# Modulation rows in half-width column groups with two selector products, and a first stage with norm sums ahead and low parts on VectorE

## The chip, the cores and the metric

The kernel runs on one NeuronCore of a Trainium2 chip. The metric is the time of one execution on the device, in microseconds (us), as the median over several runs. Five engines work side by side and are called by short names here: PE (TensorE, matrix products), DVE (VectorE), ACT (ScalarE), POOL (GpSimd) and SP (SyncE, which issues most transfers). PEld is the weight loading of PE.

## The reference

One step of a diffusion backbone with two layers, for 128 prompt tokens and 512 latent tokens of width 1024, in float32. What matters here is the modulation of each sub-layer and the first projection:

```python
def ada_modulation(cond, w_mod, b_mod):
    m = jax.nn.silu(cond) @ w_mod + b_mod
    return jnp.split(m, 6, axis=-1)

def modulate(h, shift, scale):
    return h * (1.0 + scale) + shift
...
for l in range(DEPTH):
    sh1_p, sc1_p, g1_p, sh2_p, sc2_p, g2_p = ada_modulation(cond_ctx, w_mod[l], b_mod[l])
    sh1_s, sc1_s, g1_s, sh2_s, sc2_s, g2_s = ada_modulation(cond_lat, w_mod[l], b_mod[l])
    hp = modulate(rms_norm(xp, norm_mix[l]), sh1_p, sc1_p)
    hs = modulate(rms_norm(xs, norm_mix[l]), sh1_s, sc1_s)
    # layer 0: MLA and neighbourhood attention; layer 1: grouped-query attention; then
    xp = xp + g1_p * out_p ; xs = xs + g1_s * out_s
    # FFN with sh2, sc2, g2
```

w_mod is 1024 x 6144 for each layer, so a modulation is a product of two rows (the latent and the prompt condition) with a large matrix.

## The kernel before

The 640 tokens (512 latent, 128 prompt) lie along the free axis in two halves of 320, the features on 128 partitions in eight tiles k = 0 to 7. Projections are made with three products: weights and activations are split into a high part (fp32r) and a low part, and high by high, high by low and low by high are summed (`mm3`). `unit` loads a weight block of 128 x 1024, lets ACT copy its high part, and lets DVE or POOL (argument `lo`) subtract to get the low part.

The layer-0 modulation is made in ten blocks j = 0 to 9 of 512 columns, each with two groups of columns (`MOD0`). `mod0(j, ...)` returns three pieces: two halves of row products, and an end. A half takes four of the eight k tiles; each k tile g is multiplied with its silu(condition) column pair `scol` into its own group of 32 PSUM partitions, 512 columns wide, by a matmul that uses only 32 columns of the array. After the second half ACT copies the 128 x 512 result to the tile `modsb`. The end turns it: four products of 128 columns each with `sel`, which picks and adds the four groups' rows, give `mods` with one column for each condition, and DVE adds the bias. `mkgs` then makes `gs`, the scale times the norm's weight.

The first stage makes the norm of the input and, step by step, the first three projection units wA0, wA1, wA4. For a pair of tiles k, `made(j)` runs the end of block j, `mkgs`, and `hm.make`, which gives t (`h00t`, DVE), its high part (`h00h`, ACT) and low part (`h00l`, DVE). `first` then multiplies. Of the norm, `nrm.add` sums squares on ACT and DVE into `n00acc`, and `nrm.rstd` multiplies this with ones on PE (`n00p`) and takes Ln and Exp on ACT (`n00rs`). Raw modulation rows (`mraw`) arrive in eight transfers of 1 MB. The order is written by hand: `run` queues each piece on PE behind the last matmul.

Blocks 4 to 9 stand in the neighbourhood-attention stage, one per head, as pieces m0, m1 and m2 among score, transpose and projection pieces; their raw rows arrive in quarters of 512 KB (`mod_raw`). Each fp32 matmul of the program appears as two passes in the profile, with a weight load of its own each.

Of the kernel before, what the change touches and what calls it, by code (L numbers as in the profile page):

```python
# [11 lines left out]
F32 = mybir.dt.float32  # L12
F32R = mybir.dt.float32r
AF = mybir.ActivationFunctionType
# [4 lines left out]
P = 128  # L19
# [5 lines left out]
HT = T // 2  # L25
# [23 lines left out]
def body(ctx, tc, xT, vecs, crow, wm0, wm0g, wm1, wA, wNV, wNA, wMK, wMV, wOA, wGQ, wGK, wGV, wOC,  # L49
# [3 lines left out]
    V, S, G = nc.vector, nc.scalar, nc.gpsimd  # L53
# [13 lines left out]
    main = ctx.enter_context(tc.tile_pool(name="main", bufs=1))  # L67
# [4 lines left out]
    tp = ctx.enter_context(tc.tile_pool(name="tp", bufs=4))  # L72
# [27 lines left out]
    def tmp(name):  # L100
        return tp.tile([P, T], F32, tag="t", bufs=3, name=name)

    def f(ap):
        return ap.bitcast(F32)
# [7 lines left out]
    def run(pieces):  # L112

        for piece in pieces:
            with tc.issue_after(PE.last.ins):
                piece()
# [13 lines left out]
    ident = main.tile([P, P], F32, name="ident")  # L130
# [4 lines left out]
    V.memset(eps, EPS)  # L135
    lnsc = main.tile([P, 1], F32, name="lnsc")
    V.memset(lnsc, math.log(GQA_SCALE))
    sel = main.tile([P, 2], F32, name="sel")
    V.memset(sel, 0.0)
    for g in range(4):  # L140
        V.tensor_copy(sel[32 * g:32 * g + 32, :], ident[32 * g:32 * g + 32, 32 * g:32 * g + 2])
    mods = [main.tile([P, 48, 2], F32, name=f"mods{l}") for l in range(2)]
    gs = [[main.tile([P, 8, 2], F32, name=f"gs{l}{i}") for i in range(2)] for l in range(2)]

# [3 lines left out]
    def bmod(l, j, n):  # L148
        return vec[:, V_BMOD + 48 * l + j:V_BMOD + 48 * l + j + n]

    def bc2(ap):
        return bass.AP(tensor=ap.tensor, offset=ap.offset, ap=list(ap.ap) + [[0, 2]])
# [6 lines left out]
    def load(src, n, name):  # L159
        raw = rawp.tile([P, 1024], F32, tag="raw", name=name)  # L160
        nc.sync.dma_start(raw[:, :n], src)
        return raw[:, :n]

    def unit(src, n, name, lo="v", pool=None):

        raw = load(src, n, name + "r")
        t = (pool or wp).tile([P, 2, 1024], F32R, tag="w", bufs=3, name=name)
        hi, lw = t[:, 0, :n], t[:, 1, :n]
        S.activation(hi, raw, AF.Copy)
        (V if lo == "v" else G).tensor_tensor(lw, raw, f(hi), ALU.subtract)  # L170
        return hi, lw
# [146 lines left out]
    scol = keep.tile([P, KT, 32], F32, name="scol")  # L318
# [4 lines left out]
    def mod0(j, bk, load_):  # L323

        box = []

        def part(half):
            def run():
                if half == 0:
                    box.append(bk())  # L330
                psm, rs = box[0], load_(j, half)
                for g in range(4):
                    r = rs[g // 2][:, 512 * (g % 2):512 * (g % 2 + 1)]
                    PE.matmul(psm[32 * g:32 * g + 32, :], scol[:, 4 * half + g, :], r, start=half == 0, stop=half == 1,
                              tile_position=(0, 32 * g))
                if half == 1:
                    box.append(tmp(f"modsb{j}"))
                    S.activation(box[1][:, :512], psm, AF.Copy)
            return run

        def end():
            psm, sb = box
            for i in range(4):
                PE.matmul(psm[:, 2 * i:2 * i + 2], sb[:, i * P:(i + 1) * P], sel, start=True, stop=True)
            for i, t in enumerate(MOD0[j]):
                V.tensor_tensor(mods[0][:, t:t + 2, :], psm[:, 4 * i:4 * i + 4].rearrange("p (a b) -> p a b", b=2),
                                bc2(bmod(0, t, 2)), ALU.add)
        return [part(0), part(1), end]

    def mkgs(l, i, k0=0, k1=8):  # L350
        sc = SC1 if i == 0 else SC2
        n = (V_NMIX if i == 0 else V_NFFN) + 8 * l
        V.scalar_tensor_tensor(gs[l][i][:, k0:k1, :], mods[l][:, sc + k0:sc + k1, :], 1.0, bc2(vec[:, n + k0:n + k1]),
                               ALU.add, ALU.mult)
# [114 lines left out]
    nrm = Norm("n00", D)  # L469
# [12 lines left out]
    def first(ks, us):  # L482
        for k in ks:
            for u in us:
                for c, (c0, c1) in enumerate(HALF):
                    proj(pss[u][c], *w3[u], hh, hl, [k], c0, c1, first=k == 0, last=k == KT - 1, w0=k)

    with tc.tile_pool(name="start", bufs=1) as big:
        raws = {}

        def fetch(j):
            for half in range(2):
                raws[j, half] = big.tile([P, 2, 1024], F32, tag="mraw", bufs=8, name=f"mraw{j}_{half}")
                nc.sync.dma_start(raws[j, half], wm0[j, 2 * half:2 * half + 2].rearrange("q p n -> p q n"))


        fetch(0)
        w3 = [unit(wA[0], 1024, "wA0", "g")]
        fetch(1)
        w3 += [unit(wA[i], 1024, f"wA{i}", "g") for i in (1, 4)]  # L500
        fetch(2)
        fetch(3)
        m = [mod0(j, lambda j=j: bank(f"mod{j}", "m"), lambda j, half: [raws[j, half][:, q, :] for q in range(2)]) for j in range(4)]

        def made(j):

            m[j][2]()
            mkgs(0, 0, 2 * j, 2 * j + 2)
            for k in (2 * j, 2 * j + 1):
                for i in range(2):  # L510
                    hm.make(i, nrm.rs, k)

        def rows(j):
            return m[j][:2]

        rows(0)[0]()
        run(rows(0)[1:] + [lambda i=i: nrm.rstd(i) for i in range(2)])
        run([lambda: made(0)] + rows(1))
        run([lambda: first((0, 1), [0]), lambda: made(1), lambda: first((0, 1), [1, 2])])
        run(rows(2))  # L520
        run([lambda: first((2, 3), [0]), lambda: made(2), lambda: first((2, 3), [1, 2])])
        run(rows(3))
        run([lambda: first((4, 5), [0]), lambda: made(3), lambda: first((4, 5), [1, 2])])
        run([lambda u=u: first((6, 7), [u]) for u in range(3)])
    sb = ExitStack()
# [46 lines left out]
    for kk in range(4):  # L572
        wh, wl = unit(wNV[kk], 1024, f"wnv{kk}")
        for j in range(2):
            k = 2 * kk + j
            a, b = wh[:, 512 * j:512 * (j + 1)], wl[:, 512 * j:512 * (j + 1)]
# [246 lines left out]
    for h in range(8):  # L823
        p, r = divmod(h, 2)
# [41 lines left out]
    sb = ExitStack()  # L866
# [60 lines left out]
    for h in range(8):  # L927
        p, r = divmod(h, 2)
# [390 lines left out]
    box, nxt = next_mod("h01", gs[0][1], mods[0], SH2, (op[5], op[1]))  # L1319
# [8 lines left out]
    sb = ExitStack()  # L1328
# [197 lines left out]
    box, nxt = next_mod("h11", gs[1][1], mods[1], SH2, (op[5], op[1]))  # L1526
# [168 lines left out]
```

## Time and profile before

| | |
|---|---|
| runs | 1556.8, 1561.05, 1561.08 us; median 1561.05 |
| profiled execution | 1557.29 us, span 1555.5 us, mean granted clock 0.99 |
| PE busy | 1491.6 us, 96% of the span |
| DVE, ACT, POOL busy | 1110.7, 740.8, 236.9 us |
| moved by DMA | 212.97 MB, mean 137 GB/s, 367 GB/s in the first of 40 slices |
| row products `mod<-mraw,scol` | 160 passes, 24.3 us busy, mean 648 ns of one |
| selector products `mod<-sel,modsb` | 80 passes |

Times in the profile are microseconds from the span's start. A row of the timeline has the start, the duration, the engine, the line of the kernel, the operation, out<-in tiles, and in brackets how long the engine was idle before and what ended it. Neighbouring rows of one kind are merged with a count, so a duration is then that of the run of them. In the names of tiles buffer numbers are left out (`wA` is wA1 or wA4, `h00h` any k).

### The profile page before, as it was taken

How to read it: one execution, taken by the hardware profiler on the slowest of the kernel's cores; microseconds unless marked ns; L12 is line 12 of the kernel's file. 1: busy time of each engine (PE TensorE's matmuls, PEld its weight loads, DVE VectorE, ACT ScalarE, POOL GpSimd, SP SyncE). 2: the span in 40 equal slices, each digit the busy share in tenths (PEclk: the TensorE clock that was granted, in tenths of full speed). 3: DMA queues.
4: the chain of work that ended last, by engine and by line, in shares of the span. 5: the costliest groups of instructions: out<-in, count | busy, mean ns of one | idle time of the engine just before them, and what ended most of it. 6: DMA issues, size and time to landing. Idle time of an engine off the chain costs nothing.

```text
span 1555.5 us, 25420 instructions
## 1 busy us (share of the span) xinstructions
PE 1491.6 (96%) x9868; PEld 1424.2 (92%) x9868; DVE 1110.7 (71%) x2068; ACT 740.8 (48%) x1420; POOL 236.9 (15%) x306
## 2 busy tenths in 40 slices
PE   5999989989999999999999999999989999999997
PEld 3888878879899999999999889989889999999997
DVE  5556676885779988865997787775879977743333
ACT  5445576773645555541223556663645555531221
POOL 1215444432100000000002433222100000000000
PEclk8999999999999999999999999999999999999999
DMA  9234541004165555558763211003165544457311
GB/s 367 88 112 133 176 137 57 28 14 140 36 221 180 179 170 170 168 201 320 240 227 125 88 43 35 34 15 95 38 204 186 173 133 133 143 207 264 89 41 68
DMA packets 73097, 212.97 MB, mean 137 GB/s; under 512 B 8096, under 2 KB 12976, under 8 KB 72720
## 3 DMA queue, kind: packets, MB, share of 16 engines
q1 hardware_dynamic: 70640, 205.89, 40.1%
q10 hardware_dynamic: 1920, 4.52, 0.9%
q8 instruction: 77, 1.26, 0.4%
q0 software_dynamic: 416, 0.93, 0.2%
q14 instruction: 44, 0.36, 0.1%
HBM read 182.86 MB, written 28.46 MB: 136 GB/s over the span
## 4 chain that ended last, share of the span: by engine, by line
PE 75%; DVE 12%; ACT 5%; DMA 5%; issue 2%; POOL 0%; ACTq 0%; DVEq 0%; POOLq 0%
PE fg L61 15%; PE fo L61 10%; PE fd L61 7%; PE fu L61 4%; PE gq L61 2%; PE nq L61 2%; PE mod L61 2%; PE nk L61 2%; PE go L61 1%; PE fo_2b L61 1%; PE fo_4b L61 1%; PE fo_2a L61 1%; PE fo_6b L61 1%; PE fo_4a L61 1%; PE fo_6a L61 1%
## 5 line engine op out<-in xcount | busy, mean ns | idle before, releaser
L1302 DVE SCALAR_TENSOR_TENSOR junk<-wm,cb 128x1024 bf16<-128x1024 f32 x112 | 136.7, 1220 | 21.4 <-DMA wm<-in_wm 8.4
L244 POOL TENSOR_SCALAR h10h<-h10t,gs,mods 128x320 fp32r<-128x320 f32 x4 | 5.5, 1385 | 434.8 <-DVE h10t L238 432.7
L61 PE MATMUL gq<-h10h,wgq 128*128 128x320 f32 x256 | 65.7, 315 | 0.2
L61 PE MATMUL fg<-h01q,wgu 128*128 128x320 f32 x240 | 49.6, 316 | 0.9 <-DVE h01q L287 0.4
L1065 ACT ACTIVATE wZ<-s 128x1024 fp32r<-128x1024 f32 x35 | 37.1, 1059 | 24.0 <-PE fd L61 15.7
L1065 ACT ACTIVATE wY<-s 128x1024 fp32r<-128x1024 f32 x35 | 37.1, 1060 | 22.7 <-PE fg L61 19.6
L1134 DVE TENSOR_TENSOR sg<-up,sg 128x640 f32<-128x640 f32 x35 | 28.8, 823 | 26.0 <-ACT sg L1133 26.0
L61 PEld LDWEIGHTS gq<-h10h,wgq 128*128 128x128 f32 x256 | 44.7, 188 | 1.5 <-PE gtp L65 1.0
L312 DVE SCALAR_TENSOR_TENSOR xr<-fo,mods,xr 128x320 f32<-128x320 f32 (+2 forms) x48 | 19.6, 436 | 35.0 <-PE fo L61 34.8
L1066 DVE TENSOR_TENSOR wZ<-s,wZ 128x1024 fp32r<-128x1024 f32 x35 | 42.8, 1222 | 2.4
L1066 DVE TENSOR_TENSOR wY<-s,wY 128x1024 fp32r<-128x1024 f32 x35 | 42.7, 1219 | 0.3
L61 PE MATMUL fg<-h11q,wgu 128*128 128x320 f32 x192 | 40.7, 321 | 0.9 <-DVE h11q L287 0.4
L61 PEld LDWEIGHTS fg<-h01q,wgu 128*128 128x128 f32 x240 | 38.1, 188 | 3.6 <-DVE h01q L287 2.1
L1472 ACT ACTIVATE gp<-gs,gb,rq 128x640 f32<-128x640 f32 (+1 forms) x40 | 31.9, 797 | 20.0 <-DVE gb L1471 17.1
L61 PE MATMUL mod<-mraw,scol 128*32 128x512 f32 x160 | 24.3, 648 | 17.1 <-DMA mraw<-in_wm 17.1
L61 PE MATMUL gq<-h10l,wgq 128*128 128x320 f32 x128 | 39.4, 308 | 0.0
L1133 ACT ACTIVATE sg<-fg 128x320 f32<-128x320 f32 x35 | 15.3, 438 | 46.5 <-PE fg L61 46.5
L61 PE MATMUL fg<-h11E,wW 128*128 128x320 f32 x216 | 34.7, 310 | 0.0
L61 PE MATMUL fd<-h11q,wZ 128*128 128x320 f32 x216 | 34.6, 309 | 0.0
L61 PE MATMUL fg<-h11q,wX 128*128 128x320 f32 x216 | 34.6, 309 | 0.0
L61 PE MATMUL fg<-h11N,wZ 128*128 128x320 f32 x216 | 34.6, 309 | 0.0
L61 PE MATMUL fu<-h11q,wX 128*128 128x320 f32 x216 | 34.6, 309 | 0.0
(3054 smaller groups left out, 5360.0 us busy)
## 6 DMA issues: line engine op xcount, KB each, us to landing
wm<-in_wm SPq DMA_DIRECT2D x48, 512.0 KB, 4.2
mraw<-in_wm SPq DMA_DIRECT2D x24, 512.0 KB, 4.1
mraw<-in_wm SPq DMA_DIRECT2D x8, 1024.0 KB, 15.3
wm<-in_wm0g SPq DMA_DIRECT2D x8, 512.0 KB, 4.9
x<-in_xT SPq DMA_DIRECT2D x8, 320.0 KB, 5.6
xr<-in_xT SPq DMA_DIRECT2D x8, 320.0 KB, 5.6
cb<-in_crow ACTq DMA_DIRECT2D x2, 1024.0 KB, 7.0
gt<-in_rpbp SPq DMA_DIRECT2D x8, 240.0 KB, 3.6
```

Source lines behind the costliest of these rows:

```text
L61: cls.last = nc.tensor.matmul(*a, **k)
L244: G.tensor_scalar(h[:, c0:c1], t, self.gsl[:, k, 0:1], self.ml[:, self.sh + k, 0:1], ALU.mult, ALU.add)
L312: V.scalar_tensor_tensor(xo[:, c0:c1], ps[:, c0 - o:c1 - o], ml[:, g + n, c:c + 1], xi[:, c0:c1], ALU.mult, ALU.add)
L1065: S.activation(t[:, 0, :], src, AF.Copy)
L1066: V.tensor_tensor(t[:, 1, :], src, f(t[:, 0, :]), ALU.subtract)
L1133: last = S.activation(sg[:, 0:HT], g[:, :HT], AF.Silu, scale=-1.0)
L1134: V.tensor_tensor(sg, up, sg, ALU.mult)
L1302: V.scalar_tensor_tensor(junk, raw, 1.0, cb[:, c, :], ALU.mult, ALU.mult, accum_out=mods[l][:, j0 + i, c:c + 1])
L1472: S.activation(dst, src, AF.Exp, bias=nb, scale=rq[:, j:j + 1], accum_out=ll[:, j:j + 1])
```

## The change

The four k tiles of a half no longer have a group of 32 partitions each. Column group b (0 or 1) of 256 columns and the parity of k give the group: 64 b + 32 (k mod 2). So each of the four groups receives two k tiles per half, in eight matmuls of 256 columns where there were four of 512. The result is 128 x 256; ACT copies half as many columns, into a smaller kind of tile, and two selector products replace four, with a `sel` of four columns (two conditions for two column groups).

In the first stage the norm sums `n00p` now stand ahead of the first block's row products (before: behind both halves), and the low parts of wA0, wA1 and wA4 are made by DVE instead of POOL.

```diff
-    sel = main.tile([P, 2], F32, name="sel")
+    sel = main.tile([P, 4], F32, name="sel")
...
-        V.tensor_copy(sel[32 * g:32 * g + 32, :], ident[32 * g:32 * g + 32, 32 * g:32 * g + 2])
+        V.tensor_copy(sel[32 * g:32 * g + 32, g // 2 * 2:g // 2 * 2 + 2], ident[32 * g:32 * g + 32, 32 * g:32 * g + 2])
...
                 for g in range(4):
-                    r = rs[g // 2][:, 512 * (g % 2):512 * (g % 2 + 1)]
-                    PE.matmul(psm[32 * g:32 * g + 32, :], scol[:, 4 * half + g, :], r, start=half == 0, stop=half == 1,
-                              tile_position=(0, 32 * g))
+                    for b in range(2):
+                        o = 512 * (g % 2) + 256 * b
+                        rows = slice(64 * b + 32 * (g % 2), 64 * b + 32 * (g % 2) + 32)
+                        PE.matmul(psm[rows, :256], scol[:, 4 * half + g, :], rs[g // 2][:, o:o + 256], start=half == 0 and g < 2,
+                                  stop=half == 1 and g > 1, tile_position=(0, rows.start))
                 if half == 1:
-                    box.append(tmp(f"modsb{j}"))
-                    S.activation(box[1][:, :512], psm, AF.Copy)
+                    box.append(tp.tile([P, HT], F32, tag="u", bufs=7, name=f"modsb{j}"))
+                    S.activation(box[1][:, :256], psm[:, :256], AF.Copy)
...
-            for i in range(4):
-                PE.matmul(psm[:, 2 * i:2 * i + 2], sb[:, i * P:(i + 1) * P], sel, start=True, stop=True)
+            for i in range(2):
+                PE.matmul(psm[:, 4 * i:4 * i + 4], sb[:, i * P:(i + 1) * P], sel, start=True, stop=True)
...
-        w3 = [unit(wA[0], 1024, "wA0", "g")]
+        w3 = [unit(wA[0], 1024, "wA0")]
         fetch(1)
-        w3 += [unit(wA[i], 1024, f"wA{i}", "g") for i in (1, 4)]
+        w3 += [unit(wA[i], 1024, f"wA{i}") for i in (1, 4)]
...
-        rows(0)[0]()
-        run(rows(0)[1:] + [lambda i=i: nrm.rstd(i) for i in range(2)])
+        nrm.rstd(0)
+        run([lambda: nrm.rstd(1)] + rows(0))
```

On PE, from its first product on, before (names with their numbers; `mod_230` is block 0, `mod_278` block 1):

```order
L61 MATMUL mod_230<-mraw_0_199,scol 32x512 x4
L61 MATMUL mod_230<-mraw_1_201,scol 32x512 x4
L61 MATMUL n00p_241<-n00acc,ones 128x320
L61 MATMUL n00p_245<-n00acc,ones 128x320
L61 MATMUL mod_230<-sel,modsb_239 128x2 x4
L61 MATMUL mod_278<-mraw_0_208,scol 32x512 x4
L61 MATMUL mod_278<-mraw_1_210,scol 32x512 x4
L61 MATMUL wA0a<-h00h_174,wA_205 128x320
```

and after (`mod_238` is block 0, `mod_284` block 1):

```order
L61 MATMUL n00p_230<-n00acc,ones 128x320
L61 MATMUL n00p_234<-n00acc,ones 128x320
L61 MATMUL mod_238<-mraw_0_199,scol 32x256 x8
L61 MATMUL mod_238<-mraw_1_201,scol 32x256 x8
L61 MATMUL mod_238<-sel,modsb_255 128x4 x2
L61 MATMUL mod_284<-mraw_0_208,scol 32x256 x8
L61 MATMUL mod_284<-mraw_1_210,scol 32x256 x8
L61 MATMUL wA0a<-h00h_174,wA_205 128x320
```

The norm sums moved ahead of block 0; the raw rows of block 1 still stand ahead of the first projection product.

On DVE, from the first gs to the second, before (`wA_205` is wA0, `wA_214` wA1, `wA_219` wA4; `h00t_256` and the like are t of one k and half):

```order
L353 SCALAR_TENSOR_TENSOR gs_100<-mods_98,vec 128x4
L230 SCALAR_TENSOR_TENSOR h00t_256<-x_0_114,gs_100,n00rs 128x320
L230 SCALAR_TENSOR_TENSOR h00t_260<-x_0_114,gs_100,n00rs 128x192
L230 SCALAR_TENSOR_TENSOR h00t_260<-x_0_114,gs_100,n00rs 128x128
L235 SCALAR_TENSOR_TENSOR h00l_182<-h00t_256,mods_98,h00h_174 128x320
...
L235 SCALAR_TENSOR_TENSOR h00l_183<-h00t_271,mods_98,h00h_175 128x128
L346 TENSOR_TENSOR mods_98<-mod_278,vec 128x4 x2
L353 SCALAR_TENSOR_TENSOR gs_100<-mods_98,vec 128x4
L230 SCALAR_TENSOR_TENSOR h00t_308<-x_2_118,gs_100,n00rs 128x320
```

and after:

```order
L357 SCALAR_TENSOR_TENSOR gs_100<-mods_98,vec 128x4
L231 SCALAR_TENSOR_TENSOR h00t_262<-x_0_114,gs_100,n00rs 128x320
L231 SCALAR_TENSOR_TENSOR h00t_266<-x_0_114,gs_100,n00rs 128x192
L171 TENSOR_TENSOR wA_205<-wA0r,wA_205 128x1024
L236 SCALAR_TENSOR_TENSOR h00l_182<-h00t_262,mods_98,h00h_174 128x320
...
L236 SCALAR_TENSOR_TENSOR h00l_183<-h00t_277,mods_98,h00h_175 128x128
L171 TENSOR_TENSOR wA_214<-wA1r,wA_214 128x1024
L350 TENSOR_TENSOR mods_98<-mod_284,vec 128x4 x2
L357 SCALAR_TENSOR_TENSOR gs_100<-mods_98,vec 128x4
L171 TENSOR_TENSOR wA_219<-wA4r,wA_219 128x1024
L231 SCALAR_TENSOR_TENSOR h00t_320<-x_2_118,gs_100,n00rs 128x320
```

The three low parts (L171) moved from POOL into DVE's row: one within the first pair of k, one ahead of the second block's mods, one behind its gs.

On ACT, behind the squares of the norm, before (`modsb_239`, later `modsb_255`, is block 0's copy):

```order
L338 ACTIVATE modsb_239<-mod_230 128x512
L211 ACTIVATE n00rs<-n00p_241,eps 128x320
L169 ACTIVATE wA_205<-wA0r 128x1024
L212 ACTIVATE n00rs<-n00rs 128x320
L211 ACTIVATE n00rs<-n00p_245,eps 128x320
L212 ACTIVATE n00rs<-n00rs 128x320
```

On ACT after, from the same place on:

```order
L212 ACTIVATE n00rs<-n00p_230,eps 128x320
L213 ACTIVATE n00rs<-n00rs 128x320
L212 ACTIVATE n00rs<-n00p_234,eps 128x320
L213 ACTIVATE n00rs<-n00rs 128x320
L342 ACTIVATE modsb_255<-mod_238 128x256
L170 ACTIVATE wA_205<-wA0r 128x1024
```

The copy of block 0 now stands behind all of the norm's Ln and Exp, and is half as wide.

More of the change, by code (lines that the diff above doesn't have):

```diff
@@ L342, in end @@
             psm, sb = box
-            for i in range(4):
-                PE.matmul(psm[:, 2 * i:2 * i + 2], sb[:, i * P:(i + 1) * P], sel, start=True, stop=True)
+            for i in range(2):
+                PE.matmul(psm[:, 4 * i:4 * i + 4], sb[:, i * P:(i + 1) * P], sel, start=True, stop=True)
             for i, t in enumerate(MOD0[j]):
-                V.tensor_tensor(mods[0][:, t:t + 2, :], psm[:, 4 * i:4 * i + 4].rearrange("p (a b) -> p a b", b=2),
+                V.tensor_tensor(mods[0][:, t:t + 2, :], psm[:, 0:8].rearrange("p (a i b) -> p a i b", a=2, b=2)[:, :, i, :],
                                 bc2(bmod(0, t, 2)), ALU.add)
```

## Prediction

> **What bounds the kernel now.** I read the page first, then the timeline of the first 60 us with all engines, then a table of stretches with the granted clock, then the modulation blocks in the attention stage, and last the chain of waits.
>
> ```profile
> PE 1491.6 (96%) x9868; PEld 1424.2 (92%) x9868; DVE 1110.7 (71%) x2068; ACT 740.8 (48%) x1420; POOL 236.9 (15%) x306
> L61 PE MATMUL mod<-mraw,scol 128*32 128x512 f32 x160 | 24.3, 648 | 17.1 <-DMA mraw<-in_wm 17.1
> ```
>
> TensorE (PE) is busy for 96% of the span and everything else is mostly under it, so a microsecond taken off PE, or off a wait of PE, is a microsecond off the time. Most of PE's idle time lies at the start, and that is where the change works. The timeline there (start, duration, engine, line, out<-in, count):
>
> ```profile
> 9.00 4.51 DVE L204 TENSOR_TENSOR n00acc<-n00acc,n00sq 128x320 f32<-128x320 f32 x11
> 14.23 1.94 PE L61 MATMUL mod<-mraw,scol 128*32 128x512 f32 x8 [14.23 <-DMA mraw<-in_wm]
> 16.69 1.60 PE L61 MATMUL mod<-mraw,scol 128*32 128x512 f32 x8 [0.52 <-DMA mraw<-in_wm]
> 18.21 1.34 PE L61 MATMUL n00p<-n00acc,ones 128*128 128x320 f32 x4
> 18.36 0.60 ACT L338 ACTIVATE modsb<-mod 128x512 f32<-128x512 f32 x1 [6.03 <-PE mod L61]
> 19.40 0.95 PE L61 MATMUL mod<-sel,modsb 128*128 128x2 f32 x8
> 20.44 0.23 DVE L346 TENSOR_TENSOR mods<-mod,vec 128x4 f32<-128x4 f32 x2 [6.93 <-ACT n00rs L211]
> 20.54 0.16 PEld L61 LDWEIGHTS mod<-mraw,scol 128*32 128x32 f32 x8 [0.28 <-DMA mraw<-in_wm]
> 20.61 2.35 POOL L170 TENSOR_TENSOR wA<-wA0r,wA 128x1024 fp32r<-128x1024 f32 x1 [19.30 <-ACT wA L169]
> 20.70 2.28 DVE L353 SCALAR_TENSOR_TENSOR gs<-mods,vec 128x4 f32<-128x4 f32 x1
> 23.09 1.07 PE L61 MATMUL mod<-mraw,scol 128*32 128x512 f32 x8 [1.49 <-DMA mraw<-in_wm]
> 23.09 1.15 DVE L230 SCALAR_TENSOR_TENSOR h00t<-x,gs,n00rs 128x320 f32<-128x320 f32 x3
> 24.29 0.41 PE L61 MATMUL wA0a<-h00h,wA 128*128 128x320 f32 x1
> 26.51 1.14 DVE L235 SCALAR_TENSOR_TENSOR h00l<-h00t,mods,h00h 128x320 fp32r<-128x320 f32 x3
> 28.08 0.47 PE L61 MATMUL wA0b<-h00l,wA 128*128 128x320 f32 x1
> 28.35 0.47 PE L61 MATMUL wA0b<-h00h,wA 128*128 128x320 f32 x1
> 28.61 1.70 PE L61 MATMUL mod<-sel,modsb 128*128 128x2 f32 x8
> 30.17 0.61 PE L61 MATMUL wA1a<-h00h,wA 128*128 128x320 f32 x1
> 31.03 3.67 DVE L230 SCALAR_TENSOR_TENSOR h00t<-x,gs,n00rs 128x320 f32<-128x320 f32 x4
> 35.99 1.92 PE L61 MATMUL mod<-mraw,scol 128*32 128x512 f32 x16
> 37.84 0.41 PE L61 MATMUL wA0a<-h00h,wA 128*128 128x320 f32 x1
> 39.41 0.31 PE L61 MATMUL wA0b<-h00l,wA 128*128 128x320 f32 x1
> 39.55 0.31 PE L61 MATMUL wA0b<-h00h,wA 128*128 128x320 f32 x1
> 39.70 0.95 PE L61 MATMUL mod<-sel,modsb 128*128 128x2 f32 x8
> 40.51 0.39 PE L61 MATMUL wA1a<-h00h,wA 128*128 128x320 f32 x1
> 41.02 0.16 DVE L353 SCALAR_TENSOR_TENSOR gs<-mods,vec 128x4 f32<-128x4 f32 x1
> ```
>
> Three things stand in these rows. The tiny gs at 20.70 lasts 2.28 us while POOL makes a low part (20.61 to 22.96); the same instruction at 41.02, with POOL idle, takes 0.16 us. So POOL's work holds DVE up. The first wA0 product cannot start before the raw rows that land at 23.09 have gone through PE (1.07 us), whatever DVE does. And the step from one projection product to the next is 0.27 us at 28.08, but 0.14 us at 39.41: PE runs at half speed there. The stretches confirm it (length, PE busy, granted clock, DMA share, GB/s):
>
> ```profile
> 17.81:21.23 3.42, 3.23 (x24) 1.00 1.03 410
> 21.23:24.64 3.41, 1.79 (x13) 1.00 1.03 410
> 24.64:28.05 3.41, 3.23 (x10) 0.50 1.03 410
> 31.47:34.88 3.41, 3.41 (x15) 0.50 1.02 406
> 34.88:38.29 3.41, 3.41 (x27) 1.00 1.03 383
> ```
>
> After a stretch with PE busy for 1.79 of 3.41 us the clock is 0.50, for 10.24 us (24.64 to 34.88), and full again after a stretch filled by products alone. In between lie stalls on h00h and h00l, and the selector products at 28.61, which move two columns each. DMA is full here, so the landings at 14.23, 16.69 and 23.09 stay.
>
> **The change, part by part.**
>
> *Norm sums first.* n00acc is ready at 13.51 (9.00 + 4.51). Two products on it take 1.34 us at full clock, about 2.3 at half. They now delay the first raw rows (landed 14.23), and both halves follow back to back: about 18.6 instead of 18.29 (16.69 + 1.60). The rstd pair is then done by about 17.5 and no longer sits between copy and scaling. With the shorter copy (0.45 assumed for 0.60) and four selector passes, gs comes at about 20.2 and lasts 0.16; h00t starts at 20.4, not 23.09.
>
> *Low parts by DVE.* This removes 2.35 us each from POOL, which nothing else waits for here, and adds three instructions to DVE:
>
> ```profile
> L170 DVE TENSOR_TENSOR wnv<-wnv0r,wnv x1: 1225/1225/1225, 68.3 to 68.3; 128x1024 fp32r<-128x1024 f32 x1
> ```
>
> So 1.23 us each. Block one on DVE is four triples of 1.15 (rows at 23.09 and 26.51) plus 1.23, 5.8 us: 20.4 to 26.2, where it ended at 27.65 before. PE starts at about 24.15 (0.15 earlier) and has twelve products: 12 x 0.27 = 3.2 gives 27.4 at half clock; at full clock DVE limits it to about 26.6. Before: 28.61. Gain 1.2 to 2.0, taken 1.6.
>
> *Selectors of block one.* From 28.61 to 30.17 eight passes cost 1.56. Four cost 0.78 at half clock, 0.40 at full. Gain 0.8 to 1.15, taken 1.0.
>
> *Next 24 products* (30.17 to 35.99, 5.82 us). At full clock 24 x 0.146 = 3.5. The low part of wA4 now stands on DVE behind those of wA1 and the second gs and ends near 30, which only the last products need. If the clock comes back one stretch after PE's work is dense, near 28, the 24 take about 3.7; if only near 31.5, 12 x 0.27 + 12 x 0.146 = 4.9. Gain 0.9 to 2.3, taken 2.1. Queued behind the low parts on DVE are h00t and h00l of block two: the four h00t that took 3.67 us under POOL need about 1.6 then, which pays for the 1.23 ahead of them. What is late next is the third pair of raw rows, landing near 31 by the 410 GB/s, just when PE comes for it.
>
> *Selectors of blocks two and three.* 39.70 to 40.51 is 0.81; half of it twice is 0.8.
>
> The start sums to 3.7 to 6.3 us, taken 5.5.
>
> *Attention stage, six blocks.* PE there:
>
> ```profile
> 145.80 1.68 PE L61 MATMUL mod<-mraw,scol 128*32 128x512 f32 x8
> 147.41 0.41 PE L61 MATMUL nq<-h00h,wnq 128*128 128x320 f32 x1
> 214.02 1.05 PE L61 MATMUL mod<-mraw,scol 128*32 128x512 f32 x4 [0.65 <-DMA mraw<-in_wm]
> 215.00 0.39 PE L61 MATMUL no<-nts_2h,nv 128*128 128x256 f32 x1
> 215.81 1.02 PE L61 MATMUL mod<-sel,modsb 128*128 128x2 f32 x8
> 217.59 0.33 PE L61 MATMUL npp2o<-npp2pth,nv 128*128 128x128 f32 x1 [0.77 <-ACT npp2pth L366]
> ```
>
> Five of six selector sets stand in a busy PE stream: 5 x 0.4 = 2.0. The last is followed by a wait for another copy, so it yields nothing. Raw rows come here in quarters. Where the second quarter is late (145.80, with 1.61 us to the next product, and 214.02) it now spreads over four column groups instead of two, so the tail of 0.98 (214.02 to 215.00) falls to about 0.55: 2 x 0.43 = 0.9. Some of the 2.9 turns into waits on ACT and DVE; bounds 1.0 and 2.9, taken 2.5. The shorter copies (L338) save nothing by themselves: ACT is 48% busy.
>
> *Row products.* The array streams as many columns as before: 16 passes of 512 take 1.85 us (35.99 to 37.84), although one lasts 648 ns, so four groups run at once; twice as many of 256 stream equally long. Eight weight loads go out within 0.16 us (20.54), 0.02 each, so more starts cost little. Lower bound nothing; upper bound, if the sixteen added loads of a block were not hidden at all, 16 x 0.02 = 0.32, or 2.6 us on the eight blocks on the path; taken 0.05 a block, 0.4, since the full overlap at 35.99 is the same kind of work.
>
> The Trainium skill, "TensorEngine Tiling (Array Packing)", Performance Considerations, Instruction Overhead, says that each matmul has about 60 cycles of overhead and warns against tiling a dimension that is small. By it the sixteen more passes of a block would cost an estimated 16 x 25 ns = 0.4 us, the whole selector gain, and the sum would be 4.8 us instead of 7.6. The 0.16 us for eight loads does not agree with it.
>
> *Sum.* 5.5 + 2.5 - 0.4 = 7.6 us. The profiled execution took 1557.29 (span 1555.5 and 1.8 around it), so 1549.7 against itself. The three timed runs are 1556.8, 1561.05 and 1561.08; the mean of all four is 1559.1, and I predict from that, **1551.5 us**.
>
> The Trainium skill, "TensorE: Matmul & The Clock Gate", Part 1: The HAM clock gate, says that a free-running window of 3.4 us decides on half or full clock, so its phase is drawn anew in each run. The trace agrees on the length (10.24 us is three of 3.41), and here one mostly idle stretch, not a wholly idle one, sufficed to lose the clock.
>
> **Rivals.**
>
> *More passes cost what they add* (for: twice the starts and weight loads; against: the row at 35.99, where the loads of the second half hide under the first). At 0.32 us a block the sum is 5.5 + 2.5 - 2.6 = 5.4: 1553.7 from the mean. The overhead rule of the Trainium skill cited above is of this kind.
>
> *The clock eats it.* PE now does less between 17.8 and 24.6 (norm sums moved ahead, half the selectors), so the clock may fall a stretch earlier and stay low until 34.9 as before. Then block one gains 1.2, selectors 0.8, the 24 products at 0.27 nothing (24 x 0.27 = 6.5 against 5.82, a loss of 0.6), later selectors 0.8: 2.2, and with 1.5 from attention 3.7, or 1555.4 and no difference against a median of 1561 that a measurement of this kernel tells (0.3% is 4.7 us). For it: the row 21.23:24.64. Against: dense products from 24.15 fill the stretch to 28.05, which stalls and selectors broke up before.
>
> *Slower: the column groups no longer overlap.* The new order goes round groups 0, 2, 1, 3 twice, with two matmuls for each group in one half. If a group's second pass had to start before the next group's first, the eight matmuls of a half would take nine steps of 0.21 = 1.9 instead of 1.0 us. On 17 halves (five at the start, twelve in attention) that is 15 us: 1559.1 + 15 - 8 = 1566. It decides from 0.47 us per half on. Against: two quarters that arrive apart are handled at 145.80 without such a chain, and 16 passes at 35.99 overlap fourfold across two halves.
>
> **How the numbers follow.** Chances: the forecast 0.66, passes that cost 0.11, clock 0.15, slower 0.06, and 0.02 for something else that leaves it even. The range runs from 6.3 + 2.9 off the fastest run with one half-clock stretch fewer (1.7 us), about 1546, to the smallest sum, 3.7 + 1.0 - 0.8, off the slowest pair, about 1557. Faster by over 0.3%: the forecast and most of the second case, 0.76; within 0.3%: the rest of it, the clock case and the remainder, 0.18; slower 0.06.
>
> **What would show it.** Right: gs at 20.2 lasting about 0.16; the first wA0 product near 24.15; the first wA0 product after the third block's raw rows near 33.5 instead of 37.84; fewer us at granted clock 0.50 before 40; selector sets of x4 with 0.4 us; a half of row products at 1.0 us with x16. Wrong: row halves of 1.3 us or more, PE waiting on DVE's h00l or on a low part for over 1 us between 25 and 32, half clock up to 35, or the early lead lost again at a DMA wait before 240.

## The result, and the profile after

The changed kernel takes 1550.74 us (median; 1550.31 to 1555.74), the kernel before 1561.01 in the same comparison. The ratio, which goes by the means (1551.86 and 1560.10), is 0.9947, 95% interval 0.9933 to 0.9961, about 8.3 us faster; the medians lie 10.3 us apart. The profiled execution took 1550.99 us (span 1549.2) against 1557.29 (1555.5). The page of after has:

```profile
PE 1485.5 (96%) x9988; PEld 1425.0 (92%) x9988; DVE 1109.3 (72%) x2071; ACT 738.6 (48%) x1420; POOL 230.0 (15%) x303
```

PE is busy 6.1 us less, and the span is 6.3 us shorter. The start of after, in the timeline (same columns as before):

```profile
13.17 2.50 PE L61 MATMUL n00p<-n00acc,ones 128*128 128x320 f32 x4 [13.17 <-DVE n00acc L205]
15.60 3.11 PE L61 MATMUL mod<-mraw,scol 128*32 128x256 f32 x32
18.79 0.38 ACT L342 ACTIVATE modsb<-mod 128x256 f32<-128x256 f32 x1 [2.06 <-PE mod L61]
20.20 0.16 DVE L357 SCALAR_TENSOR_TENSOR gs<-mods,vec 128x4 f32<-128x4 f32 x1
20.39 0.88 DVE L231 SCALAR_TENSOR_TENSOR h00t<-x,gs,n00rs 128x320 f32<-128x320 f32 x2
23.87 0.41 PE L61 MATMUL wA0a<-h00h,wA 128*128 128x320 f32 x1
24.70 1.14 DVE L236 SCALAR_TENSOR_TENSOR h00l<-h00t,mods,h00h 128x320 fp32r<-128x320 f32 x3
26.29 0.50 PE L61 MATMUL mod<-sel,modsb 128*128 128x4 f32 x4
26.65 0.39 PE L61 MATMUL wA1a<-h00h,wA 128*128 128x320 f32 x1
27.83 0.42 PE L61 MATMUL wA1a<-h00h,wA 128*128 128x320 f32 x1 [0.35 <-DVE wA L171]
28.03 1.23 DVE L171 TENSOR_TENSOR wA<-wA4r,wA 128x1024 fp32r<-128x1024 f32 x1
29.17 1.60 DVE L231 SCALAR_TENSOR_TENSOR h00t<-x,gs,n00rs 128x320 f32<-128x320 f32 x4
30.95 1.93 PE L61 MATMUL mod<-mraw,scol 128*32 128x256 f32 x32
32.82 0.41 PE L61 MATMUL wA0a<-h00h,wA 128*128 128x320 f32 x1
34.68 0.50 PE L61 MATMUL mod<-sel,modsb 128*128 128x4 f32 x4
35.04 0.39 PE L61 MATMUL wA1a<-h00h,wA 128*128 128x320 f32 x1
```

The tiny gs lasts 0.16 us, the four h00t 1.60 instead of 3.67, a selector set takes 0.36 us up to the next product (34.68 to 35.04) instead of 0.81, and the first product behind the third block's raw rows starts at 32.82 instead of 37.84. Thirty-two row passes of 256 columns take as long as sixteen of 512 did (1.93 at 30.95, 1.92 at 35.99). The stretches of before, with the granted clock in the third column from the end:

```profile
21.23:24.64 3.41, 1.93 (x25) 1.19 (x22) 3.41 (x9) 1.71 (x5) 0.00 (x0) 1.00 1.03 410
24.64:28.05 3.41, 2.92 (x18) 2.25 (x17) 2.66 (x9) 2.82 (x5) 0.00 (x0) 1.00 1.03 410
31.47:34.88 3.41, 3.41 (x43) 2.65 (x35) 2.09 (x7) 1.02 (x3) 0.00 (x0) 1.00 1.02 404
```

There is no half clock at the start of this execution from its first clock record, at 18.05, on. Further on I followed the lead, that is how much earlier the same first product of a tile starts than in the first profile of before. It is 5.92 us at ckv0a (53.32), 10.78 at mpp2t (312.94) and 10.83 at fu_3a (444.21), only 4.27 at fu_3b (457.27), and 6.29 at the end. So the lead grew well beyond the forecast in the attention stage, and over half of it was given back within 13 us at the start of the first FFN. There the rows of after are:

```profile
435.72 1.91 ACT L1295 ACTIVATE cb<-cb 128x2048 f32<-128x2048 f32 x1 [5.20 <-DMA cb<-in_crow]
445.56 1.23 DVE L1306 SCALAR_TENSOR_TENSOR junk<-wm,cb 128x1024 bf16<-128x1024 f32 x1 [2.58 <-DMA wm<-in_wm0g]
448.38 1.22 DVE L171 TENSOR_TENSOR wgu<-wgu_31r,wgu 128x1024 fp32r<-128x1024 f32 x1
449.65 3.03 PE L61 MATMUL fu_3a<-h01q,wgu 128*128 128x320 f32 x10 [4.00 <-DVE wgu L171]
```

and that of before:

```profile
456.32 1.72 PE L61 MATMUL fu_3a<-h01q,wgu 128*128 128x320 f32 x10
```

DVE ran these instructions in the order of the program. A product of a modulation tile (junk<-wm,cb) waited 2.58 us for its transfer, and behind it stood the low part of wgu_31, for which PE waited 4.00 us; half clock followed. In the first profile of before the same products had no wait.

### The profile page after: what moved, and what is told of

The parts are those of the page before. It is cut to its first block, busy times and chain, and to the rows that moved or that the text cites. A ratio compares the mean times of both kernels' runs of the same rounds, so it can differ in the third digit from the quotient of the medians.

```text
span 1549.2 us, 25659 instructions
## 1 busy us (share of the span) xinstructions
PE 1485.5 (96%) x9988; PEld 1425.0 (92%) x9988; DVE 1109.3 (72%) x2071; ACT 738.6 (48%) x1420; POOL 230.0 (15%) x303
## 4 chain that ended last, share of the span: by engine, by line
PE 78%; DVE 11%; ACT 6%; DMA 3%; issue 2%; POOL 0%; DVEq 0%; ACTq 0%; POOLq 0%
PE fg L61 16%; PE fo L61 10%; PE fd L61 8%; PE fu L61 4%; PE gq L61 2%; PE nk L61 2%; PE nq L61 1%; PE go L61 1%; PE mod L61 1%; PE fo_2b L61 1%; PE fo_4b L61 1%; PE fo_2a L61 1%; PE fo_4a L61 1%; PE fo_6b L61 1%; PE fo_6a L61 1%
## 5 line engine op out<-in xcount | busy, mean ns | idle before, releaser
L1171 ACT ACTIVATE p<-fd 128x320 f32<-128x320 f32 x35 | 15.3, 438 | 40.4 <-PE fd L61 40.3
```

The costliest lines, as they stand in the source:

```text
L1171: S.activation(p5, b5[:, :HT], AF.Copy)
```

## The experiments

Two times within each trace carry most of the readings: the lead at ckv0a, which is the work of the start, and the time from the first product of ckv0a to that of mpp2t, which holds the attention stage. In it every execution has two or three half-clock stretches of 3.41 us (6.8 or 10.2 us in all), in other places each time. Since PE works through most of them, I take half of their length off ("corrected"). This is an estimate, but little hangs on it: without it the means of the five stages with wide groups and of the seven with half-width groups are 263.1 and 259.2 us, with it 259.0 and 255.0.

| kernel | ratio to before (95%) | lead at ckv0a | ckv0a to mpp2t, corrected | fu_3a to fu_3b |
|---|---|---|---|---|
| before | 1 | 0 | 264.48 - 5.12 = 259.36 | 6.49 |
| before_again | 0.9994 (0.9983 to 1.0006) | -0.27 | 259.23 | 8.01 |
| fill_before | 1.0000 (0.9991 to 1.0009) | -1.40 | 258.06 | 10.21 |
| c_only | 0.9983 (0.9970 to 0.9995) | 1.81 | 258.83 | 12.66 |
| b_c | 0.9970 (0.9958 to 0.9982) | 3.28 | 259.69 | 10.48 |
| a_attn | 0.9995 (0.9985 to 1.0004) | 0.52 | 255.37 | 10.55 |
| a_only | 0.9969 (0.9957 to 0.9981) | 0.56 | 255.46 | 11.18 |
| a_b | 0.9953 (0.9938 to 0.9968) | 2.82 | 255.68 | 12.99 |
| a_c | 0.9946 (0.9932 to 0.9960) | 4.93 | 254.85 | 10.93 |
| after | 0.9947 (0.9933 to 0.9961) | 5.92 | 259.61 - 5.12 = 254.49 | 13.05 |
| copy_twice | 0.9960 (0.9946 to 0.9974) | 4.22 | 257.20 | 12.16 |
| after_p1 | 0.9921 (0.9906 to 0.9937) | 6.17 | 254.34 | 6.50 |
| after_l01 | 0.9921 (0.9907 to 0.9935) | 5.86 | 255.06 | 6.49 |

The lead at ckv0a also holds the clock of each execution's start, and that differs. The second table has, for each start, the engine of the low parts, the start of the first wA0 product, and the time of the 24 products of wA1 and wA4 that stand between the second selector set and the third block's raw rows, with the part of it at half clock:

| kernel | low parts by | first wA0 product | 24 products | of it at half clock |
|---|---|---|---|---|
| before | POOL | 24.29 | 5.82 | 4.71 |
| before_again | POOL | 25.34 | 5.09 | 3.10 |
| fill_before | POOL | 25.33 | 7.59 | 6.83 |
| a_only | POOL | 24.14 | 8.07 | 6.51 |
| a_attn | POOL | 25.75 | 5.96 | 0 |
| a_b | POOL | 25.64 | 5.33 | 0 |
| c_only | DVE | 23.88 | 5.72 | 3.41 |
| b_c | DVE | 23.46 | 5.17 | 3.27 |
| a_c | DVE | 23.66 | 4.38 | 0 |
| after | DVE | 23.87 | 4.30 | 0 |
| copy_twice | DVE | 24.97 | 3.69 | 0 |
| after_p1 | DVE | 23.83 | 4.31 | 0 |
| after_l01 | DVE | 23.65 | 4.27 | 0 |

Four of these stretches as the profile has them (before, a_only, c_only, after; start and end, length, busy time of PE, PEld, DVE, ACT and POOL, granted clock, DMA share, GB/s):

```profile
30.17:35.99 5.82, 5.82 (x26) 5.63 (x26) 5.50 (x11) 1.65 (x4) 3.12 (x2) 0.60 1.03 407
28.13:36.20 8.07, 6.49 (x27) 5.90 (x26) 7.78 (x13) 2.63 (x6) 4.68 (x2) 0.60 1.02 404
28.60:34.32 5.72, 5.49 (x26) 5.04 (x25) 5.68 (x14) 2.35 (x5) 0.00 (x0) 0.70 1.02 406
26.65:30.95 4.30, 3.95 (x26) 3.50 (x25) 4.27 (x10) 2.01 (x5) 0.00 (x0) 1.00 1.02 406
```

So both count. At full clock the 24 products take 5.3 to 6.0 us with low parts by POOL and 3.7 to 4.4 with low parts by DVE; with low parts by DVE, half clock over some 3.3 us of them makes that 5.2 to 5.7.

**a_attn: half-width groups in the attention stage alone.**

```diff
+        narrow = j >= 4
...
                 for g in range(4):
+                    if not narrow:
                         r = rs[g // 2][:, 512 * (g % 2):512 * (g % 2 + 1)]
...
+                        continue
+                    for b in range(2):
...
```

> The kernel before, with the half-width column groups and two selector products only in the six blocks of the attention stage (the four blocks of the first stage keep four groups of 512 and four selectors). Theory of the parts: the attention stage gives what my sum had, 2.5 us (1.0 to 2.9), so about -2.5 us. Rival from the trace of the changed kernel, where the lead over before grew from 5.9 us at 53 us to 12.3 at 244 us: the stage alone gives about 6 us, so -6 us, unless that is lost again at the DMA waits near 440 us (then -1 to -3 at the end, with 6 at 244 us). Rival of the clock: the lead gained in the stage came from half-clock stretches that happened to lie otherwise; then the lead at the same instruction, less what half-clock stretches cost, is 2 to 3 us.

The stage became 4.0 us shorter (corrected, 255.37 against 259.36), not 2.5, and not by the place of half-clock stretches. At the end no clear gain is left (ratio 0.9995, where about 2.5 us were expected): 4.1 us went at fu_3a, and another 3.1 between 486 and 697 us, where PE waited 3.4 us in all for ACT's and DVE's work on later FFN weights (0.55 in after). Why these waits come in some executions is not settled.

More important was a by-product. The start of this kernel is that of before, and in this execution its clock was full from 25.99 on. The lead at ckv0a is only 0.5 us, but that is not the price of the clock: the raw rows of block one ran at half pace here (3.64 us for 16 passes from 22.18), so the first wA0 product came 1.46 us later than in before. From that product to the third block's raw rows it took 9.79 us, against 11.70 in before and 10.97 in before_again, so full clock is worth some 1.2 to 1.9 us there. The rows of what held it up all the same:

```profile
29.28 2.35 POOL L174 TENSOR_TENSOR wA<-wA1r,wA 128x1024 fp32r<-128x1024 f32 x1 [5.65 <-ACT wA L173]
30.09 1.57 DVE L370 SCALAR_TENSOR_TENSOR gs<-mods,vec 128x4 f32<-128x4 f32 x1
31.59 2.39 POOL L174 TENSOR_TENSOR wA<-wA4r,wA 128x1024 fp32r<-128x1024 f32 x1
31.69 0.42 PE L61 MATMUL wA1a<-h00h,wA 128*128 128x320 f32 x1 [1.28 <-POOL wA L174]
34.03 0.55 PE L61 MATMUL wA<-h00h,wA 128*128 128x320 f32 x2 [0.47 <-POOL wA L174]
29.58:35.54 5.96, 4.21 (x26) 3.50 (x25) 5.65 (x8) 1.75 (x5) 4.40 (x2) 1.00 1.02 416
```

The 24 products take 5.96 us at full clock (last row, a stretch), where the first profile of before had 5.82 mostly at half: at full clock PE waits for the low parts of wA1 and wA4, which POOL makes one behind the other. My prediction had found nobody waiting for POOL there; in the profile that it read, the half clock hid the wait.

**a_only, b_c: the halves of the change.** a_only has the half-width groups everywhere and the old first stage, b_c the new first stage and the wide groups. The diff is that from the changed kernel to a_only; b_c is the kernel before with the same lines changed the other way.

```diff
-        w3 = [unit(wA[0], 1024, "wA0")]
+        w3 = [unit(wA[0], 1024, "wA0", "g")]
...
-        w3 += [unit(wA[i], 1024, f"wA{i}") for i in (1, 4)]
+        w3 += [unit(wA[i], 1024, f"wA{i}", "g") for i in (1, 4)]
...
-        nrm.rstd(0)
-        run([lambda: nrm.rstd(1)] + rows(0))
+        rows(0)[0]()
+        run(rows(0)[1:] + [lambda i=i: nrm.rstd(i) for i in range(2)])
```

> The kernel before, with the half-width groups and two selectors in all ten blocks, but the norm sums behind the first block's halves and low parts by POOL as before. Theory of the parts: the start gives only its selectors, 1.0 + 0.8, and not the 3.7 of POOL and of the clock, so the lead at 53 us is 1 to 2 us; with the attention stage (as in the run of that stage alone) -4 to -8 us there. Rival, passes cost: the lead at 53 us is below 0.5. Rival, the selectors alone keep the clock: no half-clock stretch from 24.6, lead at 53 us 4 to 6 us.

> The kernel before, with the norm sums first and the low parts by DVE, and the wide groups with four selectors everywhere. Theory of the parts: wA0's twelve products 1.6 and the next 24 products 2.1, so the lead at 53 us is 3.5 us (2 to 4), no more after it, and -3.5 us at the end. Rival, the clock decides and the selectors decide the clock: eight two-column passes a block leave PE idle enough that the half-clock stretch from 24.6 us stays; then the lead is 1.0 to 1.5 us. Rival, POOL decides all: 5.5 us as in the full change.

At ckv0a a_only has 0.56 us, less than the 1 to 2 expected: PE waits 1.6 us at 30.57 for wA1's low part, and the half clock from 29.69 to 36.52 stands over the rest of the 24 products, which take 8.07 us. b_c has 3.28, as expected, and nothing more in the attention stage. The two give 3.8 at ckv0a, the full change 5.92. That they need each other is not shown by this: both had half clock over the 24 products, after had none. At the end each is about 4.7 us faster than before, with intervals of 1.9 us either way, so their sum is no less than the 8.3 us of the full change.

**fill_before: PE kept busy before 23 us.**

```diff
-        run([lambda: made(0)] + rows(1))
+        run([lambda: made(0), rows(1)[0], filler, rows(1)[1]])   # filler: four products 128 x 192
```

> The kernel before, with four fp32 products of 128 x 192 put on PE between the two row halves of block one, into columns that nobody reads: PE is kept busy in its idle 1.5 us before 23.09, and nothing else is changed. Theory of the clock (a stretch of 3.41 us with PE busy for 1.79 brings half clock): the stretch is now busy for about 3 us, the clock stays full from 24.64, and although PE has more to do the lead at 53 us is 2 to 4 us. Rival (PE waits for h00h and h00l there anyway, whatever its clock): lead between -0.5 and 0.5 us.

The half clock came all the same, only later (30.44 to 37.27), and the lead is -1.40 us, outside both expectations. The 24 products, all but their start at half clock, took 7.59 us. So keeping PE busy before 23 us did not keep the clock, and what a full clock is worth this run cannot tell.

**a_c, a_b: one part of the first stage put back.** Of the lines in the last diff, a_c has the `rstd` lines put back, so the old place of the norm sums, and a_b the `unit` lines, so the low parts on POOL.

> The changed kernel with only the order of the norm sums put back (behind the first block's row halves); half-width groups, two selectors and low parts by DVE stay. Theory of the low parts (from the run with wide groups everywhere but the six attention blocks: with the clock full from 26 us on, PE still waited 1.3 us for POOL's low part of wA1 and 0.5 for that of wA4, and the 24 products still took 5.96 us): the low parts carry the start, the norm order only DVE's first start; gs comes near 21.9 instead of 20.2, DVE's first block ends near 27.8 instead of 26.2, so the lead at 53 us falls from 5.9 by 1.5 to about 4.4 us, and the time is 1.5 us above the changed kernel's. Rival, the raw rows at 23 us bound PE anyway: the lead stays at 5.5 to 5.9 and the order is worth nothing.

> The changed kernel with only the three low parts put back to POOL; half-width groups, two selectors and the norm sums first stay. Theory of the low parts: wA1's and wA4's low parts, 2.35 us each on POOL one behind the other, end about 5 us behind the copies of their high parts and hold PE up, and h00t of block two takes 3.67 us again; the 24 products take about 6 us whatever the clock, the lead at 53 us falls from 5.9 to about 2 us (1 to 3), and the time is 3 to 4 us above the changed kernel's. Rival of my prediction (the clock that is kept full carries 2.1 us of it and POOL only 1.6): if the clock stays full the lead is about 4.3 us.

The norm order is worth 1.0 us at ckv0a (no half clock in either start) and nothing that the end shows. With the low parts on POOL the lead is 3.1 us smaller (5.92 - 2.82), but 1.8 of that stands there before the first wA0 product (25.64 against 23.87): a_b's second half of raw rows landed later (23.78 against 22.87) and ran at half clock (20.78 to 27.61). The part that the clock does not touch is the 24 products, which with the clock full take 5.33 us in a_b and 4.30 in after, so 1.0 us. The rows of a_b:

```profile
20.27 3.58 DVE L231 SCALAR_TENSOR_TENSOR h00t<-x,gs,n00rs 128x320 f32<-128x320 f32 x4
30.20 0.41 PE L61 MATMUL wA1a<-h00h,wA 128*128 128x320 f32 x1 [0.63 <-POOL wA L171]
28.74:34.07 5.33, 4.22 (x27) 3.50 (x26) 5.01 (x8) 1.19 (x4) 3.76 (x2) 1.00 1.02 402
```

At the end a_b is about 1 us behind the changed kernel (0.9953 against 0.9947, less than the intervals), where 3 to 4 were expected.

**c_only: the low parts alone**, the `unit` lines of the first stage without the argument "g" and nothing else.

> The kernel before with only the three low parts moved from POOL to DVE; wide groups, four selectors and norm sums behind block 0 stay. With half-width groups the same move gave 4.93 - 0.56 = 4.4 us of lead at 53 us (without the norm order) and 5.92 - 2.82 = 3.1 (with it). Theory of the low parts (it is the main term of the start by itself): a lead of 2.0 to 3.5 us at 53 us, and 2 to 4 us at the end. Rival (the terms need each other: without the shorter selectors the move only passes the wait on): below 1 us.

1.81 us at ckv0a, a little under the range, and 2.7 us at the end (0.9983). With the half-width groups the same move gives 4.4 (4.93 - 0.56), but this difference holds the clock too: the 24 products of a_only ran mostly at half clock, those of c_only for 3.41 us, those of a_c at full. Whether the low parts pay more once the selectors are shorter stays open.

**copy_twice: a longer copy.**

```diff
                     S.activation(box[1][:, :256], psm[:, :256], AF.Copy)
+                    S.activation(box[1][:, :256], psm[:, :256], AF.Copy)
```

> The changed kernel, with ACT's copy of each modulation block made twice, so that it takes about as long as the old 512-wide one (0.6 us) or a little longer. My prediction said that the shorter copies save nothing by themselves. Theory from the traces: ahead of the selectors PE waited 0.36 us after the last product before and 0.12 after in three sets of the attention stage, 1.19 and 0.94 in a fourth, so PE waits for the copy and the second copy costs 0.3 us in four to six of the six sets there and some 0.3 at the start: 1.5 to 2 us less lead at 323 us than the changed kernel, and about that at the end. Rival (the prediction): nothing, within 0.5 us at 323 us.

The lead at mpp2t falls from 10.78 to 6.37: 1.7 us are lost at the start and 2.2 to 2.7 in the attention stage (257.20 against a mean of 255.04 with single copies, or 254.49 in after). The loss at the start proves little, as half clock stood there from 22.07 to 28.90. In the attention stage PE's waits ahead of the six selector sets sum to 3.46 us, against 1.21 in after. It is more than expected because another ACT instruction slipped between the two copies:

```profile
136.27 0.39 ACT L342 ACTIVATE modsb<-mod 128x256 f32<-128x256 f32 x1 [0.39 <-PE mod L61]
136.68 0.48 ACT L675 ACTIVATE nk<-nk 64x384 fp32r<-64x384 f32 x1
137.19 0.38 ACT L343 ACTIVATE modsb<-mod 128x256 f32<-128x256 f32 x1
137.63 0.61 PE L61 MATMUL mod<-sel,modsb 128*128 128x4 f32 x4 [0.75 <-ACT modsb L343]
```

So the size is that of a copy ending 0.9 us later, but the dependence is shown: PE stands still until the copy is there.

**before_again: a second profile of before.**

> The kernel before once more, unchanged, for a second profile of it. In the first one PE did not wait ahead of fu_3a (454 us), where all five other profiles have a wait of 2.0 to 4.0 us and a half-clock stretch behind it. Theory: that profile was a lucky execution by about 4 us (1557.3 against a median of 1560 to 1561), and this one shows a wait of about 2 us there. Rival: the kernel before has no wait there, and every other kernel has it because its PE comes earlier; then there is none here and the time is near 1557.

PE waits there now, in the list of waits:

```profile
PE fu_4a L61 <- DVE wgu L170: 1.9, 1, 1.9
PE fu_3a L61 <- DVE wgu L170: 1.3, 1, 1.3
```

The wait belongs to before too, and its size changes from one execution to the next. The first profile, with 1.5 at fu_4a alone, was a lucky one. But this one, at 1557.07, is no slower, so its luck at fu_3a does not explain the 1557.3.

**after_p1: one tile fewer ahead of wgu_31.**

```diff
-                    lambda kind, i: (0, 0, 0, 2, 3)[i] if kind == "fb" and i < 5 else ...
+                    lambda kind, i: (0, 0, 0, 1, 4)[i] if kind == "fb" and i < 5 else ...
```

> The changed kernel with one number pair of a plan changed: of the modulation tiles that DVE makes from loaded rows in the first FFN, one instead of two stands in step three and four instead of three in step four. In the changed kernel's trace two of them, held up by a late transfer, stand ahead of wgu_31's low part on DVE, and PE waits 4.0 us for it at 449.65 and then runs 6.8 us at half clock. Theory: the wait falls below 1.5 us and the half-clock stretch goes, so 3 to 5 us faster than the changed kernel (about 1546 to 1547.5). Rival: the wait moves to the next step (fu_4a, where four tiles now stand), and the time stays within 1 us of the changed kernel's.

1548.1 us, 2.6 under the changed kernel, a little less than expected (3 to 5). DVE comes to wgu_31 at once, PE runs on, and the clock of 443 to 457 us is 1.00 in it and 0.76 in after (the two stretches, after_p1 first); 1.15 us wait at fu_4a:

```profile
443.76 1.22 DVE L171 TENSOR_TENSOR wgu<-wgu_31r,wgu 128x1024 fp32r<-128x1024 f32 x1 [0.41 <-ACT wgu L170]
445.06 1.72 PE L61 MATMUL fu_3a<-h01q,wgu 128*128 128x320 f32 x10
462.43 2.75 PE L61 MATMUL fu_4a<-h01q,wgu 128*128 128x320 f32 x17 [1.15 <-DVE wgu L171]
443.00:457.00 14.00, 14.00 (x96) 13.80 (x95) 9.23 (x14) 3.10 (x6) 0.00 (x0) 1.00 0.63 201
443.00:457.00 14.00, 10.00 (x52) 9.61 (x51) 7.11 (x10) 3.26 (x5) 0.00 (x0) 0.76 0.60 202
```

It is faster than both kernels: the ratio to before is 0.9921 (0.9906 to 0.9937), and its six runs (1546.84 to 1549.39) all lie below the eight of after. after_l01, with the same plan numbers, has no wait at fu_3a in the first FFN either.

**after_l01: the same in the second FFN.**

```diff
-    side = mod_side([(1, wm1[G2:], G2)], lambda kind, i: int(kind == "n" or i > 1))
+    side = mod_side([(1, wm1[G2:], G2)], lambda kind, i: int(kind == "n" or i > 4))
```

> The changed kernel with the plan numbers of the run after_p1, and the same idea in the second FFN: there its loaded modulation tiles begin after step four instead of after step one, so that no 512 KB transfer of theirs and no DVE work of theirs stands ahead of wgu_31's low part and of wu_4's copy. Every profile so far has a wait of 3.2 to 5.0 us there (fu_3a near 1150 us), with 3.4 to 6.8 us of half clock behind it. Theory: this wait falls below 1.5 us and half of the stretch goes, 3 to 5 us faster than after_p1 (1543 to 1545). Rival (transfers of the weights themselves are late there, whatever stands ahead of them): within 1 us of 1548.

1548.37 us: nothing more. The list of waits from 1100 to 1260 us has:

```profile
PE fg L61 <- ACT u L1175: 3.5, 5, 0.9
PE fu_3a L61 <- ACT wgu L170: 1.3, 1, 1.3
PE fu_3a L61 <- DVE wgu L171: 1.1, 1, 1.1
```

The 3.7 us at fu_3a became 2.4, and five waits of up to 0.9 us appeared in the later steps into which the tiles were moved. That the moved tiles make these waits is argued from their place, not shown.

## Why the prediction came true, point by point

The time forecast, 1551.5 us, is 0.8 us off the median. That is partly luck: two errors of opposite sign, more work saved than forecast and a loss in the FFN that was not foreseen.

- *Start, 5.5 us forecast, 5.9 measured.* gs at 20.20, h00t at 20.39, the first wA0 product at 23.87, the low part of wA4 done at 29.26 and 32.82 behind the third block's rows are as forecast or slightly earlier. The twelve products ended at 26.29, a gain of 2.3 for 1.6 (range to 2.0), the selectors gave 1.2 for 1.0 (eight passes take 0.81 at full clock, in a_attn, so 0.45 of it is their number and the rest the half clock of the first profile), the 24 products 1.5 for 2.1, blocks two and three 0.9 for 0.8.
- *The step that failed in it is the low parts.* "If the clock comes back ... the 24 take about 3.7" put the whole gain of the 24 products on the clock, and POOL's low parts were called something "which nothing else waits for here". But at full clock the 24 took 5.96 us in a_attn and 5.33 in a_b, where POOL made the low parts, and 4.30 in after; the clock and the faster low parts are needed together. In after, too, PE waited for wA1's low part (0.35 us, at 27.83), which the sum had at nothing; the gain is 1.5 and not 2.1. That nothing waits for POOL holds in the one profile that I had, since at half clock PE was late itself. A row of that profile would have told it:

```profile
30.93 2.37 POOL L170 TENSOR_TENSOR wA<-wA4r,wA 128x1024 fp32r<-128x1024 f32 x1
```

  wA4's low part was not there before 33.3, and the sixteenth of the 24 products needs it; fifteen at full clock would have brought PE there by 32.4 (30.17 + 15 x 0.146). What is not settled is whether the change itself keeps the clock. The starts of after, after_p1, after_l01 and a_c had none of the half clock, those of b_c, c_only and copy_twice had some.
- *Selectors in the attention stage.* 2.0 us forecast. The six sets, each up to the next product, sum to 6.14 us before and 3.84 after, so 2.3. But three of the five sets that the prediction had in a busy stream stand behind a wait for their copy.
- *The shorter copies "save nothing by themselves" is wrong.* That ACT is busy for 48% says nothing of a chain in which PE, ACT and PE follow each other. Before and after:

```profile
140.72 0.60 ACT L338 ACTIVATE modsb<-mod 128x512 f32<-128x512 f32 x1 [0.41 <-PE mod L61]
141.37 1.05 PE L61 MATMUL mod<-sel,modsb 128*128 128x2 f32 x8
134.61 0.39 ACT L342 ACTIVATE modsb<-mod 128x256 f32<-128x256 f32 x1 [0.39 <-PE mod L61]
135.05 0.61 PE L61 MATMUL mod<-sel,modsb 128*128 128x4 f32 x4
```

  The selectors start 0.05 us behind the copy's end both times, so what the copy loses in length PE loses in wait: 0.24 us in each of three sets, 0.7 in all. The sixth set gives most of it back, as it now waits 0.5 us for its copy.
- *Attention stage in all: 2.5 forecast (1.0 to 2.9), 4.0 measured*, the difference between the mean of five old stages (259.0) and of seven new ones (255.0). It is the one of the two large terms that lies outside its bounds. By the means of these traces the selector sets give 2.2 of it and the raw rows 1.6: the twelve halves, each up to the next product, sum to 13.7 us in the old stages and 12.1 in the new. These are the tails of late quarters, which I had at 0.9. In the old stages they cost 0.8 to 2.6 us, in the new ones 0.4 at most, so this is the term that was sized too small. The waits ahead of the selectors sum to 1.1 us in the old and 1.2 in the new, so they did not fall in all. The rest, 0.8 gained behind the last set and some 0.6 lost between, I could not assign, nor why late quarters became so rare.
- *More passes cost nothing.* 0.4 was put down, 0 measured: a half takes 1.00 us with 16 passes of 256 as with 8 of 512. The rival in which they cost, and the rival in which the groups no longer overlap (1.9 us a half) are refuted by that. The rule of the Trainium skill, "TensorEngine Tiling (Array Packing)", Performance Considerations, Instruction Overhead, by which a block would have cost an estimated 0.4 us more, does not show in this form of matmul either.
- *Not foreseen: the FFN.* I had looked for a lost lead before 240 us; it was lost at 449. The wait is there before as well (0 and 1.3 us at fu_3a, then 1.5 and 1.9 at fu_4a), but is 4.0 with the half clock behind it in after. That a shorter wait there is worth time is shown by after_p1; why it was longer in nearly all kernels with a lead (2.0 to 4.0 at fu_3a) is not, since the transfers are issued at the same distance from PE's work in both. cb, 1 MB, was ready 8.4 to 9.0 us after its issue in ten of the profiles, 5.9 and 7.5 in the two of before and 7.8 in after_l01.

So 5.9 and 4.0 make 9.9 us of work saved, of which some 1.6 do not reach the end; the forecast had 7.6 and no such loss. The 5.9 is not one execution's: the three traces with the new start have 5.9 to 6.2 at ckv0a, the three with the old one (before, before_again, a_attn) -0.3 to 0.5.

## What to carry to other kernels

A profile at reduced clock hides the waits that full clock would show: before putting a gain on the clock, compute for each engine that feeds PE when it would be done, and take the later of the two. Price a copy between two steps of one engine by the gap ahead of the second step, whatever share of the span the copying engine is busy. And when a lead is gained early, look for the next place where PE hangs on an in-order queue with a transfer in it: here moving one tile of side work there was worth as much as a third of the change. And before two leads are compared, compare the clock of the two starts: here it differed between several of the runs set against each other.

## What the runs showed of the hardware

- Twice as many row passes of half the width take the same time: 1.00 us for a half at full clock, and 1.94 for both forms ahead of the first clock record (8 of 512 at 14.01 in a_attn, 16 of 256 at 13.79 in a_c).
- Beside a POOL subtraction, DVE's `SCALAR_TENSOR_TENSOR` did not run slower but stood still until POOL was done. A gs on 128 x 4 elements took 0.30 to 2.28 us and ended 0.01 to 0.03 us behind POOL's instruction in all eleven cases of six traces (0.16 us without POOL); an h00t that fell into one took 2.52 to 2.64 instead of 0.55 and ended 0.34 to 0.35 behind it in all seven. Four h00t took 3.58 to 3.70 so, against 1.60. The `TENSOR_TENSOR` of mods on 128 x 4 elements took 0.15 to 0.16 either way.
- How long PE is busy in a 3.41 us stretch did not decide the clock of the next. Half clock followed stretches with 1.79 us busy (before, 21.23) and 2.16 (a_only, 26.27); full clock stayed after 2.01 (after, 21.46). The 1.79 us that the prediction calls mostly idle are over half of the stretch.
- The same start took 11.70 us from the first wA0 product to the third block's raw rows in before, with 10.24 us of half clock, 10.97 in before_again, with 6.83, and 9.79 in a_attn, with none.
